# Zero-padding the low part of the keys to 128 rows, and regrouping ScalarE and VectorE in the turning of x

## The chip, the cores and the metric

The kernel runs on one core of one Trainium2 chip. The metric is the device time of one execution in microseconds (us). Three runs of the kernel before took 1794.21, 1795.99 and 1801.98 us; their median, 1795.99 us, is the time before.

## The reference

Two layers over 256 tokens of 2048 channels, in float32. The first layer projects the normalized input once and feeds a convolution module and a sparse attention with 16 heads in 4 groups; the second is a causal pooling mixer. After each comes an MLP. The part that the change touches is the scores of the attention, and the transposition of the residual x ahead of the MLPs and of the pooling layer:

```python
sc = jnp.einsum('bqgrd,bngd->bgrqn', qb, kc) * scale            # compressed keys
ss = jnp.einsum('bqgrd,bgqkld->bgrqkl', qb, ks_sel) * scale     # selected keys
sw = jnp.einsum('bqgrd,bkgd->bgrqk', qb, kwb) * scale           # window keys
...
x = x + even_mixer(x, ...)
x = x + mlp(x, ...)      # rmsnorm(x) @ w1, squared ReLU, @ w2
x = x + odd_mixer(x, ...)
x = x + mlp(x, ...)
```

With 256 tokens all blocks are selected and the window covers everything, so that the selected and the window branch are two plain causal attentions with keys of their own.

## The kernel before

**Products in two halves.** A float32 product is made from operands rounded to a faster format (F32R) and their remainders: a tensor `hi` holds the rounded values, `lo` the difference, and three matmuls (hi by hi, hi by lo, lo by hi) stand for one. ScalarE rounds (`nc.scalar.activation(hi, ..., AF.Copy)`), VectorE subtracts. The weights stream from HBM in units of 1 MB (`wraw`), are split into `whi` and `wlo` (L147, and L78, which is the line of every VectorE instruction, since a helper counts their cost), and are used two units later. Matmuls stand under L194, transposes on TensorE under L232.

**Order of the work.** Each engine runs its instructions in the order in which the program issues them. In the mixing part, `unit_cols` (L365) multiplies one unit of weights with xT in four quarters, and after each quarter `beside` (L356) issues a quarter of the split of a later unit, then as many taps of the convolution (`ctile`, VectorE) as the meter `vector.t` allows against the time counted for TensorE, then one entry of the list `steps`. In the part with the queries (L859, 8 units of q) the entries are the steps of the attention.

**A step of the attention** (`step`, L678). There are 32, one for each pair of heads, half and token block; step s transposes the softmax numerators of step s-2 (`T<-ident,p`), forms the scores of step s (`scores`, L609), and multiplies the values of step s-4 (`PV`). The scores of both branches are three matmuls into one bank `S`: the query `q`, whose 128 rows hold the rounded query in one half and its remainder in the other, with `kk2`, which holds the rounded keys twice (L616); the rounded half of the query alone, 64 rows, with `klo`, the remainder of the keys (L617); and a product with the identity that adds the causal mask (L618, `cmaskr`). A step with the second token block is wide (512 columns, both branches over 256 keys), one with the first is narrow (256 columns). VectorE takes the maximum (`nb`), ScalarE the exponentials (`p`), and two steps later TensorE transposes them. `klo` and `kk2` are written in `keys_values` (L475), in the stretch from 134 to 174 us: two units for each of two branches.

**Buffers.** Tiles of one tag rotate through `bufs` buffers, and the writer waits for the readers of the tile that had the buffer before. `row` has 4 buffers, `ln` has 3.

**Turning x** (`turn_x`, L242). Four calls ahead of the first MLP (from 367 us), four ahead of the pooling layer and four ahead of the second MLP (from 1043 to 1125 us). A call turns 512 channels: 8 transposes into two banks of PSUM, then for each of 4 tiles a rounding by ScalarE (L254) and a difference by VectorE, both reading the bank and scaling by `g`. Between the calls, in the pooling part, VectorE adds the pooled parts to x (`pt`, then `x<-x,pt`), and the next transposes wait for that x.

Of the kernel before, what the change touches and what calls it, by code (L numbers as in the profile page):

```python
# [27 lines left out]
F32 = mybir.dt.float32  # L28
F32R = mybir.dt.float32r
AF = mybir.ActivationFunctionType  # L30
ALU = mybir.AluOpType
# [3 lines left out]
P = 128  # L35
S = 256
# [143 lines left out]
def trunk(ctx: ExitStack, tc: tile.TileContext, a: dict, out: bass.AP, dump: dict | None = None):  # L180
    nc = tc.nc
# [6 lines left out]
    vector = Meter(nc.vector)  # L188
    pe = [0.0]

    def mm(out, w, x, **kw):
        n = int(np.prod(x.shape[1:]))
        pe[0] += max(4 * n / 2400, 0.214) if x.dtype == F32 else max(n / 2400 + 0.0025, 0.107)
        nc.tensor.matmul(out, w, x, **kw)  # L194
# [39 lines left out]
    def split_evac(hi, lo, src):  # L234
        nc.scalar.activation(hi, src, AF.Copy)
        vector.tensor_sub(lo, src, hi.bitcast(F32))
# [5 lines left out]
    def turn_x(dc, g0, bank):  # L242

        xT[dc] = act.tile([P, 4, 512], F32R, tag="xT", bufs=4, name="xT")
        for h in range(2):
            t = bank().rearrange("p (f t) -> p f t", f=2)
            for f in range(2):
                d = (4 * dc + 2 * h + f) * P
                for tok in range(2):
                    transpose(t[:, f, tok * P:(tok + 1) * P], x[:, tok, d:d + P])  # L250
            for f in range(2):
                dt = 4 * dc + 2 * h + f
                o, g = xT[dc][:, 2 * h + f], vec[:, g0 + dt:g0 + dt + 1]
                nc.scalar.activation(o[:, 0:256], t[:, f], AF.Copy, scale=g)  # L254
                vector.scalar_tensor_tensor(o[:, 256:512], t[:, f], g, o[:, 0:256].bitcast(F32),
                                            op0=ALU.mult, op1=ALU.subtract)

    def by_token(acc, X, hi, lo, first, last, between=None, outer=False):

# [13 lines left out]
    with ExitStack() as mx:  # L273
        mix = mx.enter_context(tc.tile_pool(name="mix", bufs=1, side="right", reuse_waits="tile"))
# [38 lines left out]
            vector.tensor_add(sq[0][:, 0:n], sq[0][:, 0:n], sq[0][:, n:2 * n])  # L313
        nc.scalar.activation(identr, ident, AF.Copy)
        r0 = const.tile([P, 2], F32, name="r0")
        rbc = mix.tile([P, S], F32, name="rbc")
        pss = acc1(2)

        def start_steps():
# [107 lines left out]
        for ct in range(1, 8):  # L427
            g, a_ = acc1(), acc1()
# [16 lines left out]
        for i in range(2):  # L445
            t = mix.tile([P, KT, P], F32, tag="q8", bufs=2, name="w1")
# [5 lines left out]
        for i in range(2):  # L452
            t = mix.tile([P, 512], F32, tag="tt", bufs=3, name="wgl")[:, 0:384]
# [7 lines left out]
        for pr in range(2):  # L461
            for i in range(2):
                acc = acc1()
# [5 lines left out]


        kk2 = mix.tile([P, 2, 2, 2, 256], F32R, name="kk2")
        klo = mix.tile([P, 2, 2, 256], F32R, name="klo")
        v = mix.tile([P, 2, 2, 256], F32, name="v")

        def keys_values(br):  # L475
            for i in range(2):
                acc = acc1()
                unit_cols(acc)
                hi = mix.tile([P, 256], F32R, tag="row", bufs=4, name="khi")
                split_evac(hi, klo[:, i, br], acc)  # L480
                for h in range(2):
                    for o in range(2):
                        nc.scalar.activation(kk2[64 * o:64 * o + 64, i, h, br], hi[64 * h:64 * h + 64].bitcast(F32), AF.Copy)
            accs = [acc1() for _ in range(2)]
            for u in range(2):
                hi, lo = W.next(8)
                for tok in range(2):
                    for k in range(8):
                        mm3_toks(accs[tok], xT[2 * u + k // 4], k % 4, hi[:, k], lo[:, k], tok,
                                 u == 0 and k == 0, u == 1 and k == 7)  # L490
                        if k % 4 == 3:
                            beside(2 * tok + k // 4)
            for tok in range(2):
                nc.scalar.activation(v[:, br, tok], accs[tok], AF.Copy)
# [105 lines left out]
        qT, Pt, Tt, SM, PV, PC, PP, ab = {}, {}, {}, {}, {}, {}, {}, {}  # L600
# [8 lines left out]
        def scores(s):  # L609

            j, half, tok = of_step(s)
            n = P * (tok + 1)
            b = slice(64 * half, 64 * half + 64)
            S_ = bank("S")[:, 0:2 * n].rearrange("p (b k) -> p b k", b=2)
            q = qT[j][:, half, tok * P:(tok + 1) * P]
            mm(S_, q, kk2[:, j // 4, half, :, 0:n], start=True, stop=False)  # L616
            mm(S_, q[b], klo[b, j // 4, :, 0:n], start=False, stop=False)  # L617
            mm(S_[:, :, n - P:n], identr, cmaskr[:, None].to_broadcast([P, 2, P]), start=False, stop=True)  # L618
            if s % 4 == 0:
                SM[j] = const.tile([P, 2, 2, 2], F32, tag="sums", bufs=4, name="sums")  # L620
            nb = const.tile([P, 2], F32, tag="nb", bufs=3, name="nb")
            p = mix.tile([P, 2, n], F32, tag="p", bufs=3, name="p", padded_shape=[P, 2, 256])
            vector.tensor_reduce(nb, S_, axis=AX, op=ALU.max, negate=True)

            def exps():
                for br in range(2):
                    nc.scalar.activation(p[:, br], S_[:, br], AF.Exp, bias=nb[:, br:br + 1],
                                         accum_out=SM[j][:, tok, half, br:br + 1])
                return p
            Pt[s] = exps  # L630
# [64 lines left out]
        def cmp_scores(j):  # L695
            m, r = divmod(j, 4)
            transposed()
            sc = (ab.pop(j)[:, 256:384] if j < 7 else bank("T")[:, 0:128]).rearrange("p (t h i n) -> p t h i n", t=2, h=2, i=2)
            for tok in range(2):
                for half in range(2):  # L700
                    mm(sc[:, tok, half], qT[j][:, half, tok * P:(tok + 1) * P], kcT[:, m, half],
                       start=(tok == 0 and half == 0), stop=True, skip_group_check=True)
            if r == 0:

                PC[m] = mix.tile([P, 2, 2, 4, 16], F32, tag="scm", bufs=1, name="scm")
            lo = const.tile([P, 2, 2, 16], F32, tag="sclo", bufs=2, name="sclo")
            nc.scalar.activation(lo, sc[:, :, :, 1], AF.Copy)
            pc = PC[m][:, :, :, r]
            vector.tensor_add(pc, sc[:, :, :, 0], lo)
            vector.tensor_add(pc, pc, madd[:, :, None].to_broadcast([P, 2, 2, 16]))  # L710

        def cmp_max(m):
            PP[m] = mix.tile([P, 2, 2, 4, 32], F32, tag="pp", bufs=1, name="pp")
            nc.gpsimd.memset(PP[m], 0.0)
            cm = const.tile([P, 16], F32, tag="cm", bufs=2, name="cm")
            s3 = PC[m].rearrange("p t h r n -> p (t h r) n")
            vector.tensor_reduce(cm, s3, axis=AX, op=ALU.max)
            vector.tensor_tensor(s3, s3, cm[:, :, None].to_broadcast([P, 16, 16]), op=ALU.subtract)
# [44 lines left out]
        ln = {}  # L763
# [95 lines left out]
        for j in range(8):  # L859
# [19 lines left out]
            m = j // 4  # L879
# [540 lines left out]
```

## Time and profile before

| | |
|---|---|
| runs | 1794.21, 1795.99, 1801.98 us |
| median | 1795.99 us |
| the profiled execution, its time | 1794.04 us |
| the same, span from first to last instruction | 1792.3 us |
| granted TensorE clock, mean | 0.998 |
| TensorE busy | 1767.5 us, 99% of the span |
| VectorE busy | 1517.0 us, 85% |
| ScalarE busy | 1088.4 us, 61% |
| GpSimd busy | 57.8 us, 3% |

The profile is of one execution. PE is TensorE's matmuls, PEld its loads of stationary operands, DVE is VectorE, ACT ScalarE, POOL GpSimd. Matmuls are pipelined, and the end of one is modelled; what a matmul takes from the engine is therefore read from the distance between its start and the start of the next. A TensorE that is 99% busy by its records can still lose time between two starts.

### The profile page before, as it was taken

To read this page: it belongs to the slowest core of one execution; us is meant where nothing else is said; L and a number is where in the kernel's file an instruction comes from. 1 tells how busy PE (TensorE), PEld (TensorE's weight loads), DVE (VectorE), ACT (ScalarE), POOL (GpSimd) and SP (SyncE) were. 2 spreads that over 40 slices of the span, in tenths; PEclk is the share of its full clock that TensorE was granted. 3 is DMA by queue.
4 is the path that set the end of the run, shared out by engine and by line. 5 is a ranking of instruction groups with operands and counts; after the bars stand their busy time and mean duration, and the time that the engine had idled before them with its cause. 6 is when DMAs were issued, how large, how long until landed. Compare 5 with 4: busy or idle time off the path is not lost.

```text
span 1792.3 us, 28698 instructions
## 1 busy us (share of the span) xinstructions
PE 1767.5 (99%) x11726; PEld 1599.5 (89%) x11726; DVE 1517.0 (85%) x1884; ACT 1088.4 (61%) x1626; POOL 57.8 (3%) x78
## 2 busy tenths in 40 slices
PE   9999999999999999999999999999999999999997
PEld 7999988889898988999898988989889998989885
DVE  6998896865889898988989868698999889898984
ACT  4446565546666666666656655766666666666663
POOL 1000000000000000000000000000000000000000
PEclk9999999999999999999999999999999999999999
DMA  7654322545787787878787764678877787878872
GB/s 276 238 187 143 117 75 103 202 183 200 239 250 257 255 263 238 251 235 278 236 285 235 217 227 162 212 253 255 256 238 247 233 291 236 270 235 258 245 239 104
DMA packets 58052, 399.89 MB, mean 223 GB/s; under 512 B 6560, under 2 KB 6960, under 8 KB 10816
## 3 DMA queue, kind: packets, MB, share of 16 engines
q1 hardware_dynamic: 47760, 333.47, 48.4%
q0 software_dynamic: 8576, 61.43, 18.4%
q10 hardware_dynamic: 1584, 3.16, 0.5%
q8 instruction: 92, 1.51, 0.3%
q14 instruction: 40, 0.33, 0.0%
HBM read 395.93 MB, written 2.10 MB: 222 GB/s over the span
## 4 chain that ended last, share of the span: by engine, by line
PE 72%; DVE 22%; ACT 3%; issue 2%; DMA 1%; ACTq 0%; POOLq 0%; SPq 0%; DVEq 0%
PE acc L194 68%; DVE wlo L78 11%; DVE z L78 3%; DVE s L78 3%; PE S L194 2%; DVE x L78 2%; ACT whi L147 1%; PE PV L194 1%; PE T L232 1%; DVE xT L78 1%; DVE f L78 1%; DMA xraw<-in_xT 0%; ACT xT L254 0%; ACT t L1018 0%; ACT sq L997 0%
## 5 line engine op out<-in xcount | busy, mean ns | idle before, releaser
L194 PE MATMUL acc<-xT,whi 128*128 128x256 f32 x4992 | 874.1, 279 | 0.3
L194 PEld LDWEIGHTS acc<-xT,whi 128*128 128x128 f32 x4992 | 765.8, 188 | 10.5 <-DVE xT L78 0.7
L78 DVE TENSOR_TENSOR wlo<-wraw,whi 128x1024 fp32r<-128x1024 f32 (+1 forms) x552 | 604.0, 1124 | 146.4 <-ACT whi L147 145.3
L194 PE MATMUL acc<-xT,wlo 128*128 128x256 f32 x2496 | 694.9, 278 | 0.0
L147 ACT ACTIVATE whi<-wraw 128x1024 fp32r<-128x1024 f32 (+1 forms) x552 | 514.5, 973 | 94.7 <-PE acc L194 66.2
L194 PEld LDWEIGHTS acc<-xT,wlo 128*128 128x128 f32 x2496 | 470.8, 189 | 0.0
L194 PE MATMUL acc<-whi,s 128*128 128x512 f32 x960 | 318.6, 393 | 2.7 <-DVE s L78 1.6
L78 DVE TENSOR_TENSOR wlo<-z,whi 128x1024 fp32r<-128x1024 f32 x224 | 266.6, 1216 | 48.3 <-ACT whi L147 47.2
L147 ACT ACTIVATE whi<-z 128x1024 fp32r<-128x1024 f32 x224 | 230.6, 1054 | 93.8 <-DVE z L78 75.9
L194 PE MATMUL acc<-whi,f 128*128 128x512 f32 x864 | 283.1, 392 | 0.0
L194 PEld LDWEIGHTS acc<-whi,s 128*128 128x128 f32 x960 | 179.5, 188 | 42.0 <-DVE s L78 7.4
L1017 ACT ACTIVATE t<-acc 128x256 f32<-128x256 f32 x128 | 48.8, 382 | 252.9 <-PE acc L194 252.4
L194 PE MATMUL acc<-wlo,s 128*128 128x512 f32 x480 | 190.8, 398 | 1.2
L194 PEld LDWEIGHTS acc<-whi,f 128*128 128x128 f32 x864 | 162.5, 188 | 32.1
L194 PE MATMUL acc<-wlo,f 128*128 128x512 f32 x432 | 169.5, 392 | 0.0
L78 DVE SCALAR_TENSOR_TENSOR x<-acc,r,x 128x512 f32<-128x512 f32 x156 | 115.5, 742 | 13.5 <-PE acc L194 13.5
L194 PEld LDWEIGHTS acc<-wlo,s 128*128 128x128 f32 x480 | 90.2, 188 | 28.1 <-DVE wlo L78 9.7
L78 DVE SCALAR_TENSOR_TENSOR ctile<-ctile,cw 128x256 f32<-128x256 f32 x240 | 101.6, 476 | 0.0
L194 PEld LDWEIGHTS acc<-wlo,f 128*128 128x128 f32 x432 | 81.2, 188 | 16.0
L1062 ACT ACTIVATE s<-s 128x512 fp32r<-128x512 f32 x56 | 35.4, 632 | 72.1 <-DVE s L78 72.1
L78 DVE TENSOR_TENSOR z<-z,b 128x1024 f32<-128x1024 f32 x56 | 65.9, 1218 | 0.0
L78 DVE TENSOR_TENSOR z<-z,wraw 128x1024 f32<-128x1024 f32 x56 | 65.8, 1214 | 0.0
(205 smaller groups left out, 1366.4 us busy)
## 6 DMA issues: line engine op xcount, KB each, us to landing
wraw<-in_ws SPq DMA_DIRECT2D x254, 1024.0 KB, 6.1
z<-in_ws SPq DMA_DIRECT2D x28, 1024.0 KB, 7.5
b<-in_ws SPq DMA_DIRECT2D x28, 1024.0 KB, 4.8
b<-in_ws POOLq DMA_DIRECT2D x28, 1024.0 KB, 8.9
z<-in_ws POOLq DMA_DIRECT2D x28, 1024.0 KB, 8.0
xraw<-in_xT SPq DMA_DIRECT2D x4, 512.0 KB, 7.6
wraw<-in_ws SPq DMA_DIRECT2D x8, 256.0 KB, 7.6
w<-in_cmp_w POOLq DMA_DIRECT2D x2, 1024.0 KB, 7.4
```

Source lines behind the costliest of these rows:

```text
L78: return fn(*args, **kw)
L147: nc.scalar.activation(hi[:, c], raw[:, c], AF.Copy)
L194: nc.tensor.matmul(out, w, x, **kw)
L232: nc.tensor.transpose(out, src, ident[0:n, 0:n])
L1017: nc.scalar.activation(out, acc, AF.Relu)
L1062: nc.scalar.activation(F[tag][:, :, 0:P], src(), AF.Copy)
```

## The change

The remainder of the keys gets a tile of twice the size with one more index, the half (the group of 64 channels). For each half, the 64 rows of the other half are zero, and the matmul takes all 128 rows of the query; the zeros meet the query's remainder. GpSimd sets the zeros once, and VectorE writes each remainder in two instructions of 64 rows. Three tiles that had buffers of their own get buffers of a rotating tag: `rbc` and `scm` in `row`, `pp` in `ln`. In `turn_x` the four differences are issued after the four roundings of the call.

```diff
     def turn_x(dc, g0, bank):
         xT[dc] = act.tile([P, 4, 512], F32R, tag="xT", bufs=4, name="xT")
+        rest = []
...
                 nc.scalar.activation(o[:, 0:256], t[:, f], AF.Copy, scale=g)
-                vector.scalar_tensor_tensor(o[:, 256:512], t[:, f], g, o[:, 0:256].bitcast(F32),
-                                            op0=ALU.mult, op1=ALU.subtract)
+                rest.append(lambda o=o, t=t[:, f], g=g: vector.scalar_tensor_tensor(
+                    o[:, 256:512], t, g, o[:, 0:256].bitcast(F32), op0=ALU.mult, op1=ALU.subtract))
+        for r in rest:
+            r()
...
-        rbc = mix.tile([P, S], F32, name="rbc")
+        rbc = mix.tile([P, S], F32, tag="row", bufs=4, name="rbc")
...
-        klo = mix.tile([P, 2, 2, 256], F32R, name="klo")
+        klo = mix.tile([P, 2, 2, 2, 256], F32R, name="klo")
+        for h in range(2):
+            nc.gpsimd.memset(klo[64 - 64 * h:128 - 64 * h, :, h].bitcast(F32), 0.0)
...
-                split_evac(hi, klo[:, i, br], acc)
+                nc.scalar.activation(hi, acc, AF.Copy)
+                for h in range(2):
+                    b = slice(64 * h, 64 * h + 64)
+                    vector.tensor_sub(klo[b, i, h, br], acc[b], hi[b].bitcast(F32))
...
-            b = slice(64 * half, 64 * half + 64)
...
-            mm(S_, q[b], klo[b, j // 4, :, 0:n], start=False, stop=False)
+            mm(S_, q, klo[:, j // 4, half, :, 0:n], start=False, stop=False)
...
-                PC[m] = mix.tile([P, 2, 2, 4, 16], F32, tag="scm", bufs=1, name="scm")
+                PC[m] = mix.tile([P, 2, 2, 4, 16], F32, tag="row", bufs=4, name="scm")
...
-            PP[m] = mix.tile([P, 2, 2, 4, 32], F32, tag="pp", bufs=1, name="pp")
+            PP[m] = mix.tile([P, 2, 2, 4, 32], F32, tag="ln", bufs=3, name="pp")
```

TensorE issues the same matmuls in the same order as before, 32 of them with 128 rows for 64. On VectorE, where the second branch of the keys is written (`keys_values(1)`, L475), the program issues the following; `klo` is the remainder of the keys, `ctile` a tap of the convolution, `wlo` the split of a unit of weights. Before:

```order
L78 TENSOR_TENSOR klo<-acc,khi 128x256
L78 SCALAR_TENSOR_TENSOR ctile<-ctile,cw 128x256 x2
L78 TENSOR_TENSOR wlo<-wraw,whi 128x1024
L78 SCALAR_TENSOR_TENSOR ctile<-ctile,cw 128x256 x4
L78 TENSOR_TENSOR wlo<-wraw,whi 128x1024
```

With the change:

```order
L78 TENSOR_TENSOR klo<-acc,khi 64x256 x2
L78 SCALAR_TENSOR_TENSOR ctile<-ctile,cw 128x256
L78 TENSOR_TENSOR wlo<-wraw,whi 128x1024
L78 SCALAR_TENSOR_TENSOR ctile<-ctile,cw 128x256 x4
L78 TENSOR_TENSOR wlo<-wraw,whi 128x1024
```

The remainder is two instructions, the meter counts both, and one tap moves to a later quarter; after this the taps of the attention's part stand one place later than before.

In `turn_x` no engine's own order changes; what each instruction waits for does. On ScalarE, the first two calls ahead of the first MLP (L254 is the rounding, PE_49 and DVE_49 are the signals of TensorE and VectorE). Before:

```order
L254 ACTIVATE xT<-acc,vec 128x256 [waits PE_49]
L254 ACTIVATE xT<-acc,vec 128x256 [waits DVE_49]
L254 ACTIVATE xT<-acc,vec 128x256 [waits PE_49]
L254 ACTIVATE xT<-acc,vec 128x256 [waits DVE_49]
L147 ACTIVATE whi<-wraw 128x512 x2
L147 ACTIVATE whi<-wraw 128x512 [waits DMAHW2_49,PE_49,Activation_49]
```

With the change:

```order
L255 ACTIVATE xT<-acc,vec 128x256 [waits PE_49]
L255 ACTIVATE xT<-acc,vec 128x256
L255 ACTIVATE xT<-acc,vec 128x256 [waits PE_49]
L255 ACTIVATE xT<-acc,vec 128x256
L147 ACTIVATE whi<-wraw 128x512 x2
L147 ACTIVATE whi<-wraw 128x512 [waits DMAHW2_49,DVE_49,PE_49]
```

The second rounding of each bank no longer waits for VectorE's difference in that bank. On VectorE, the differences of the first call with what stands around them, before (each waits for a rounding):

```order
L78 TENSOR_TENSOR wlo<-wraw,whi 128x512 [waits DMAHW1_49,Activation_49]
L78 TENSOR_TENSOR wlo<-wraw,whi 128x512 [waits Activation_49]
L78 SCALAR_TENSOR_TENSOR xT<-acc,vec,xT 128x256 [waits Activation_49] x4
L78 TENSOR_TENSOR wlo<-wraw,whi 128x512 [waits Activation_49] x2
L78 TENSOR_TENSOR x<-xt,acc 128x512
```

and with the change:

```order
L78 TENSOR_TENSOR wlo<-wraw,whi 128x512 [waits DMAHW1_49,Activation_49]
L78 TENSOR_TENSOR wlo<-wraw,whi 128x512 [waits Activation_49]
L78 SCALAR_TENSOR_TENSOR xT<-acc,vec,xT 128x256 [waits PE_49,Activation_49]
L78 SCALAR_TENSOR_TENSOR xT<-acc,vec,xT 128x256
L78 SCALAR_TENSOR_TENSOR xT<-acc,vec,xT 128x256 [waits PE_49,Activation_49]
L78 SCALAR_TENSOR_TENSOR xT<-acc,vec,xT 128x256
L78 TENSOR_TENSOR wlo<-wraw,whi 128x512 [waits Activation_49] x2
L78 TENSOR_TENSOR x<-xt,acc 128x512
```

The first difference of a bank now waits for both roundings of that bank, and the second for nothing.

## Rows read from the trace of the kernel before

**Rows 1.** The page: busy time of the engines (part 1), and the chain of work that ended last, by engine (part 4).

```profile
PE 1767.5 (99%) x11726; PEld 1599.5 (89%) x11726; DVE 1517.0 (85%) x1884; ACT 1088.4 (61%) x1626; POOL 57.8 (3%) x78
...
PE 72%; DVE 22%; ACT 3%; issue 2%; DMA 1%; ACTq 0%; POOLq 0%; SPq 0%; DVEq 0%
```

**Rows 2.** Busy time by stretch: length of the stretch, then PE, PEld, DVE, ACT, POOL busy (with the number of instructions), granted clock, DMA share, GB/s. The first stretch is the projection of the convolution's channels, the second the attention, the third the part of the attention in which taps of the convolution still run beside it.

```profile
36.00:134.00 98.00, 98.00 (x829) 97.87 (x828) 93.10 (x168) 44.56 (x62) 5.14 (x11) 1.00 0.62 231
...
194.00:300.00 106.00, 104.30 (x747) 90.84 (x746) 87.25 (x203) 67.49 (x214) 0.53 (x1) 1.00 0.27 95
...
194.00:274.00 80.00, 79.98 (x587) 70.72 (x586) 71.75 (x168) 51.03 (x159) 0.53 (x1) 1.00 0.26 93
```

**Rows 3.** Timeline of TensorE, one wide step (from 225.26) and one narrow step (from 228.73): start, duration, engine, line, instruction, out<-in, rows*columns of the stationary operand, out shape, count, and idle time before it.

```profile
225.26 0.48 PE L194 MATMUL S<-kk,q 128*128 128x512 f32 x1
...
225.67 0.49 PE L194 MATMUL S<-klo,q 64*128 64x512 f32 x1
...
226.09 0.19 PEld L194 LDWEIGHTS S<-cmaskr,identr 128*128 128x128 f32 x1 [0.24 <-issue]
226.09 0.39 PE L194 MATMUL S<-cmaskr,identr 128*128 128x256 f32 x1
...
226.31 1.00 PE L194 MATMUL PV<-v,tt 128*128 128x64 f32 x8
...
228.73 0.36 PE L194 MATMUL S<-kk,q 128*128 128x256 f32 x1
...
229.02 0.38 PE L194 MATMUL S<-klo,q 64*128 64x256 f32 x1
...
229.33 0.39 PE L194 MATMUL S<-cmaskr,identr 128*128 128x256 f32 x1
...
229.55 0.55 PE L194 MATMUL PV<-v,tt 128*128 128x64 f32 x4
```

**Rows 4.** Timeline of TensorE where every matmul has 128 rows: the product with w_out, 512 columns (the first of these follows PV), and a unit of the queries, 256 columns.

```profile
227.56 0.39 PE L194 MATMUL acc<-xT,whi 128*128 128x256 f32 x2
...
227.79 0.28 PE L194 MATMUL acc<-xT,wlo 128*128 128x256 f32 x1
...
290.85 0.48 PE L194 MATMUL acc<-whi,yo 128*128 128x512 f32 x1
291.16 0.39 PE L194 MATMUL acc<-wlo,yo 128*128 128x512 f32 x1
291.39 0.63 PE L194 MATMUL acc<-whi,yo 128*128 128x512 f32 x2
```

**Rows 5.** Who VectorE waited for between 195 and 274 us: instruction <- releaser: us in total, times, longest.

```profile
DVE nb L78 <- PE S L194: 3.0, 6, 0.8
DVE q L78 <- ACT q L870: 1.5, 1, 1.5
DVE o_tok L78 <- PE T L194: 1.1, 1, 1.1
DVE scm L78 <- ACT sclo L707: 0.6, 1, 0.6
```

**Rows 6.** Timeline of three engines around 251 to 259 us: `scm` reads the bank into which the next unit's `acc` is formed; `nb` and `p` belong to the scores whose `p` is transposed at 258.69.

```profile
251.57 0.21 DVE L78 TENSOR_TENSOR scm<-acc,sclo 128x64 f32<-128x64 f32 x1
...
253.75 0.69 DVE L78 TENSOR_REDUCE nb<-S 128x2 f32<-128x512 f32 x1
...
254.39 0.48 PE L194 MATMUL acc<-xT,whi 128*128 128x256 f32 x2
...
256.61 0.47 ACT L627 ACTIVATE p<-S,nb 128x256 f32<-128x256 f32 x1
...
258.69 0.60 PE L232 MATMUL T<-ident,p 128*128 128x128 f32 x4
```

**Rows 7.** Instructions by tile, with shortest, median and longest duration in ns, first and last start (`klo`, and `q`, an instruction of VectorE with 64 rows and 256 columns); the page's group of the convolution's taps (busy us, mean ns); and who VectorE waited for between 134 and 190 us.

```profile
L194 PE MATMUL S<-klo,q x32: 379/437/501, 194.7 to 298.3; 64*128 64x512 f32 x16, 64*128 64x256 f32 x16
L78 DVE TENSOR_TENSOR klo<-acc,khi x4: 410/420/426, 135.0 to 172.7; 128x256 fp32r<-128x256 f32 x4
...
L78 DVE SCALAR_TENSOR_TENSOR q<-acc,q x16: 417/422/426, 193.8 to 285.9; 64x256 fp32r<-64x256 f32 x16
...
L78 DVE SCALAR_TENSOR_TENSOR ctile<-ctile,cw 128x256 f32<-128x256 f32 x240 | 101.6, 476 | 0.0
...
DVE wlo L78 <- ACT whi L147: 8.8, 7, 2.8
```

**Rows 8.** Timeline of ScalarE and VectorE in one call of `turn_x` in the pooling part.

```profile
1103.39 0.48 ACT L254 ACTIVATE xT<-acc,vec 128x256 fp32r<-128x256 f32 x1 [1.04 <-PE acc L232]
...
1106.26 0.47 DVE L78 SCALAR_TENSOR_TENSOR xT<-acc,vec,xT 128x256 fp32r<-128x256 f32 x1
...
1106.77 0.84 ACT L254 ACTIVATE xT<-acc,vec 128x256 fp32r<-128x256 f32 x2 [2.90 <-DVE xT L78]
1107.28 0.88 DVE L78 SCALAR_TENSOR_TENSOR xT<-acc,vec,xT 128x256 fp32r<-128x256 f32 x2 [0.54 <-ACT xT L254]
...
1108.70 0.48 DVE L78 SCALAR_TENSOR_TENSOR xT<-acc,vec,xT 128x256 fp32r<-128x256 f32 x1 [0.55 <-ACT xT L254]
```

**Rows 9.** Who TensorE's loads waited for between 1040 and 1130 us (total us, times, longest); `acc L232` are the transposes of x, `acc L194` the matmuls that read xT.

```profile
PEld acc L232 <- DVE x L78: 1.5, 2, 1.0
PEld acc L194 <- DVE xT L78: 0.7, 2, 0.3
```

## The prediction

> **What bounds the kernel now.** I read the page first, then busy time by stretch, then timelines of the two places that the change touches. TensorE is busy for 99% of the span, and the chain that ended last runs through it for 72% and through VectorE for 22% [rows 1]. So a saving counts only if it shortens TensorE's own list or a wait of TensorE. The stretches say what kind of bound it is [rows 2]. From 36 to 134 us TensorE starts 829 matmuls in 98.00 us, 0.118 us each, and its loads are busy for 97.87 us: nothing else fits there. In the attention, 194 to 300 us, it is busy for 104.30 of 106 us, but starts only 747 matmuls, 0.142 us each, and its loads are busy for 90.84 us. Something there takes time that is neither a matmul nor a load, and the timeline shows what [rows 3].
>
> A wide step: the starts of `kk`, `klo`, `cmaskr` and the first `PV` lie at 225.26, 225.67, 226.09 and 226.31, so the three score matmuls take 0.41, 0.42 and 0.22 us, 1.05 in all. A narrow step takes 0.29, 0.31 and 0.22, 0.82 in all. Where every matmul has 128 rows, one with 512 columns takes 0.23 us (291.16 to 291.39), or 0.31 where it comes first after matmuls of another kind (290.85 to 291.16), and one with 256 columns 0.115 us (two in 0.23, from 227.56) [rows 4]. The excess stands at the two passages into the 64 rows of `klo` and out of them. The load ahead of `cmaskr` starts together with its matmul, after 0.24 us of "issue" [rows 3]; elsewhere a load runs during the matmul before.
>
> **The change part by part.**
>
> *The scores.* TensorE's list is the same but for the 64 rows, which become 128. If all three are then like the matmuls of [rows 4], a wide step takes 0.31 + 0.23 + 0.115 = 0.66 us for 1.05, and a narrow one, with the same 0.08 for coming first, 0.08 + 3 x 0.115 = 0.43 for 0.82. Both save 0.39 us, and 32 steps [rows 7] save 12.5 us. Bounds: `cmaskr` repeats its moving operand for both branches, and its 0.22 us may be its own; then a step saves 0.29 us, and all 9.3. If nothing of 0.08 is left, 0.41 to 0.42 and 13.3. I take 12.5: since the load ahead of `cmaskr` starts only with its matmul, its 0.22 us holds a load that otherwise is hidden.
>
> [...]
>
> *VectorE falls behind.* This is the cover that wears thin. Between 194 and 274 us, where taps of the convolution still run, VectorE is busy for 71.75 of 80 us [rows 2], and its waits over a noticeable length are 3.0 us for scores and 3.2 for other things [rows 5]. So its list takes 80 - 6.2 = 73.8 us. The moved tap adds 0.42 us (101.6 us over 240) [rows 7]: 74.2. TensorE's list becomes 80 - 24 x 0.39 = 70.6 us, with 24 of the 32 steps ahead of 274. VectorE is then 3.6 us late at the end, and what counts is whether TensorE sees it. Worst is 254 us: 19 steps have saved 7.4 us, plus 0.4, less the waits that VectorE can drop until then (3.0 + 0.6): 4.2 us behind. The margin there: `nb` ends at 254.44, two exponentials of 0.47 follow, and with starting up `p` could be ready at 255.6; its transposes start at 258.69 [rows 6], 3.1 us later, of which a narrow step between takes 0.39. So about 1.5 us of waiting. `scm` gives the same: it ends at 251.78, the matmul that needs its bank starts at 254.39 [rows 6], 2.6 us of margin less a wide step, against 3.8 us of lateness: 1.6. I take 1.6 us, once, since TensorE's waiting gives VectorE the time back, and after 274 VectorE's list gets short. Bounds: 0 (if `p` and `scm` come sooner than that) to 6.8 us (if VectorE can drop only its 3.0 us of waits for scores: it then leaves 3.0 - 0.4 = 2.6 us of the 24 steps' 9.4).
>
> *TensorE's own rate.* A dense run of 256-column matmuls goes at 0.118 us each [rows 2], one after a pause at 0.115 [rows 4]. With the pauses gone, some 200 matmuls of the units between the steps may go at the slower rate: 200 x 0.003 = 0.6 us lost. Bounds 0 and 1.
>
> *Writing the remainders.* Four instructions of 128 rows (0.42 us) become eight of 64. The nearest row is `q`, 64 rows and 256 columns, 0.42 us too [rows 7], so 4 x 0.42 = 1.7 us more on VectorE between 134 and 174 us. VectorE waits there for ScalarE's roundings for 8.8 us [rows 7], and these cover it: 0. If the cover were gone, +1.7. GpSimd's zeros are two instructions more on an engine whose 78 took 57.8 us in all [rows 1], 0.7 us each, and no instruction of VectorE or TensorE waits for GpSimd that did not before: 0, and 1.5 us if all of it were on the path. The three moved tiles add waits on tiles read long before: 0. ScalarE's and VectorE's new waits for older signals (`whi` now waits for DVE_49) are for instructions that lie units back: 0.
>
> *The turning of x.* In a late call VectorE's four differences run from 1106.26 to 1109.18, 2.92 us, with two waits of 0.54 for a rounding that itself waited for a difference; ScalarE had made the first rounding at 1103.39 and then sat still for 2.90 us [rows 8]. With all roundings done, four differences take 3 x 0.40 + 0.48 = 1.7 us: 1.2 us less on VectorE. Where VectorE is there first, it starts a rounding later (0.37, from two in 0.84) and ends about 0.9 sooner (one alternation for each bank less). What TensorE loses around these calls is small: 1.5 us for x and 0.7 us for xT between 1040 and 1130 us, four waits [rows 9]. Three of the four calls from 1095 us on give 1.2 us each, more than these 2.2 us need. I take 2.0; bounds 0 and 2.2. The calls before the first MLP cost TensorE nothing now, and give nothing.
>
> **Sum.** Against the profiled execution's 1794.04 us: -12.5 + 1.6 + 0.6 - 2.0 = -12.3, giving 1781.7. The median of the runs is 1795.99, 1.95 higher, and less 12.3 it is 1783.7. I forecast **1783 us**. The parts' bounds, short of VectorE taking over, give savings from 15.5 down to 6.7 us, both ends unlikely since they need every part on one side; I give this case 1779 to 1788.
>
> **The rivals.**
> *VectorE takes over.* Its 3.2 us of other waits between 194 and 274 cannot be dropped [rows 5], and TensorE gains there only 2.6 us; the 8 later steps give 3.1 and the turning 2.0: -7.7, 1788.3 from the median. For it: VectorE's 71.75 of 80 us. Against: its results are due two steps later, not at once.
> [...]
> *Slower: VectorE's list sets the pace at both places.* It has 1.7 us more between 134 and 174, 0.4 of the tap, and starts five calls of the turning (1079 to 1125 us) 0.37 later each, 1.9: +4.0, 1800. This decides only if VectorE's 8.8 us of waits there turn out as chains that it cannot shorten, if TensorE's saving all turns into waits for VectorE, and if the later differences aren't sooner. [Rows 8] speak against the last.
> *The change in the turning does nothing*, because no engine's order changes, only what is waited for: then 2.0 us are missing, 1785, inside the forecast's own range.
>
> **How the numbers follow.** Forecast 0.70, VectorE takes over 0.14, pauses stay 0.12, slower 0.04. About 0.5%, 9 us, is what a measurement of this kernel can tell from no change, so faster means below 1787. The forecast holds that for nearly all its range (0.68), VectorE's case for some (0.06): faster 0.74; the rest of them and the pauses' case: within, 0.22; slower 0.04. The range reaches from 1778 (full savings, and a run a little below) to 1790 (VectorE's case whole), and leaves out the pauses' and the slower case, 0.16.
>
> **What would show it.** In the changed profile `klo` has 128*128 rows, the "issue" time ahead of `klo` and `cmaskr` is gone, and a wide step takes about 0.66 us from `kk` to the next start, a narrow one 0.43. If these stand at 1.05 and 0.82, the account of the passages is wrong. Busy time from 194 us to the end of the attention should shrink by some 11 us with the same matmuls; TensorE should show one or two new waits, 1 to 2 us, for `p` or `scm` near 245 to 260, and VectorE's waits for scores should vanish. More waits than 4 us there mean that VectorE took over. In `turn_x` the two roundings of a bank should follow each other, and TensorE's waits for x and xT near 1100 us should be under 0.5 us.

## The result, and the profile after

The changed kernel takes **1777.9 us** (median; 1775.47 to 1779.22), the kernel before, measured beside it, 1795.1 us (1790.65 to 1801.98). The ratio is 0.991, with an interval from 0.9892 to 0.9928: 13 to 19 us faster. The profiled execution took 1777.96 us, with a span of 1776.2 us. Forecast were 1783 us and a saving of 12.3; the saving in the two profiled spans is 16.1.

The page of the changed kernel: busy time, and the chain that ended last by engine.

```profile
PE 1752.6 (99%) x11726; PEld 1595.4 (90%) x11726; DVE 1518.5 (85%) x1888; ACT 1084.6 (61%) x1626; POOL 59.7 (3%) x80
...
PE 78%; DVE 18%; ACT 2%; issue 1%; DMA 1%; ACTq 0%; POOLq 0%; SPq 0%; DVEq 0%
```

TensorE is busy for the same 99% of its span, with the same 11726 matmuls [rows 1]: the time has gone out of the distances between them. Busy time by stretch (columns as in [rows 2]):

```profile
36.00:134.00 98.00, 98.00 (x829) 97.87 (x828) 95.42 (x168) 44.58 (x62) 7.04 (x13) 1.00 0.62 231
194.00:300.00 106.00, 104.32 (x816) 99.58 (x815) 95.37 (x224) 71.45 (x226) 0.53 (x1) 1.00 0.30 105
```

In the first stretch TensorE's work did not move; VectorE is busy for 2.3 us more there with the same 168 instructions, which is taken up below. From 194 to 300 us TensorE now starts 816 matmuls where it started 747, and its loads are busy for 99.58 us where it was 90.84 [rows 2]. One wide and one narrow step (TensorE's timeline, columns as in [rows 3]):

```profile
227.20 0.48 PE L194 MATMUL S<-kk,q 128*128 128x512 f32 x1
227.52 0.39 PE L194 MATMUL S<-klo,q 128*128 128x512 f32 x1
227.75 0.28 PE L194 MATMUL S<-cmaskr,identr 128*128 128x256 f32 x1
227.87 1.00 PE L194 MATMUL PV<-v,tt 128*128 128x64 f32 x8
...
230.28 0.37 PE L194 MATMUL S<-kk,q 128*128 128x256 f32 x1
230.48 0.28 PE L194 MATMUL S<-klo,q 128*128 128x256 f32 x1
230.60 0.28 PE L194 MATMUL S<-cmaskr,identr 128*128 128x256 f32 x1
230.72 0.55 PE L194 MATMUL PV<-v,tt 128*128 128x64 f32 x4
```

From `kk` to `PV` it is 0.67 and 0.44 us, where it was 1.05 and 0.82 [rows 3]. The whole attention, from the first `kk` to the last `cmaskr`, first of before, then of the change:

```profile
194.31 0.50 PE L194 MATMUL S<-kk,q 128*128 128x512 f32 x1
...
298.57 0.39 PE L194 MATMUL S<-cmaskr,identr 128*128 128x256 f32 x1
```

```profile
194.44 0.50 PE L194 MATMUL S<-kk,q 128*128 128x512 f32 x1
...
286.55 0.28 PE L194 MATMUL S<-cmaskr,identr 128*128 128x256 f32 x1
```

That is 104.26 us, and then 92.11: **12.15 us less**. The second place is the turning of x. The transposes of the fourth and of the eighth of the late groups, before and then with the change:

```profile
1078.33 1.03 PE L232 MATMUL acc<-ident,x 128*128 128x128 f32 x8
...
1119.80 1.09 PE L232 MATMUL acc<-ident,x 128*128 128x128 f32 x8
```

```profile
1065.96 1.03 PE L232 MATMUL acc<-ident,x 128*128 128x128 f32 x8
...
1105.47 1.04 PE L232 MATMUL acc<-ident,x 128*128 128x128 f32 x8
```

41.47 us became 39.51, 1.96 less, and the 0.7 us of waits for xT [rows 9] behind these calls are gone too: some **2.5 us**. In a call ScalarE and VectorE no longer alternate; this is the call at 1091 us:

```profile
1090.87 1.20 ACT L255 ACTIVATE xT<-acc,vec 128x256 fp32r<-128x256 f32 x3
...
1092.74 1.65 DVE L78 SCALAR_TENSOR_TENSOR xT<-acc,vec,xT 128x256 fp32r<-128x256 f32 x4
```

The four differences take 1.65 us in one piece, where they took 2.92 [rows 8]. The two places make 14.6 us of the 16.1; where the rest lies is a question for the experiments.

### The profile page after: what moved, and what is told of

It is laid out like the page before. It is cut to its first block, busy times and chain, and to the rows that moved or that the text cites. A ratio compares the mean times of both kernels' runs of the same rounds, so it can differ in the third digit from the quotient of the medians.

```text
span 1776.2 us, 28729 instructions
## 1 busy us (share of the span) xinstructions
PE 1752.6 (99%) x11726; PEld 1595.4 (90%) x11726; DVE 1518.5 (85%) x1888; ACT 1084.6 (61%) x1626; POOL 59.7 (3%) x80
## 4 chain that ended last, share of the span: by engine, by line
PE 78%; DVE 18%; ACT 2%; issue 1%; DMA 1%; ACTq 0%; POOLq 0%; SPq 0%; DVEq 0%
PE acc L194 73%; DVE wlo L78 9%; DVE z L78 3%; DVE s L78 3%; PE S L194 2%; DVE x L78 2%; PE PV L194 1%; ACT whi L147 1%; PE T L232 1%; PE acc L232 1%; DVE f L78 0%; DMA xraw<-in_xT 0%; ACT t L1026 0%; DMA ident<-in_ident 0%; ACT t L1025 0%
## 5 line engine op out<-in xcount | busy, mean ns | idle before, releaser
L194 PE MATMUL acc<-xT,whi 128*128 128x256 f32 x4992 | 872.1, 279 | 0.0
L194 PEld LDWEIGHTS acc<-xT,whi 128*128 128x128 f32 x4992 | 764.8, 188 | 10.1
L194 PE MATMUL acc<-xT,wlo 128*128 128x256 f32 x2496 | 694.0, 278 | 0.0
L194 PEld LDWEIGHTS acc<-xT,wlo 128*128 128x128 f32 x2496 | 470.7, 189 | 0.0
L194 PE MATMUL acc<-whi,s 128*128 128x512 f32 x960 | 318.5, 393 | 2.8 <-DVE s L78 1.6
L194 PE MATMUL acc<-whi,f 128*128 128x512 f32 x864 | 283.0, 392 | 0.0
L194 PEld LDWEIGHTS acc<-whi,s 128*128 128x128 f32 x960 | 179.3, 188 | 42.2 <-DVE s L78 7.5
L194 PE MATMUL acc<-wlo,s 128*128 128x512 f32 x480 | 190.8, 397 | 1.1
L194 PEld LDWEIGHTS acc<-whi,f 128*128 128x128 f32 x864 | 162.4, 188 | 32.2
L194 PE MATMUL acc<-wlo,f 128*128 128x512 f32 x432 | 169.4, 392 | 0.0
L194 PEld LDWEIGHTS acc<-wlo,s 128*128 128x128 f32 x480 | 90.1, 188 | 28.2 <-DVE wlo L78 9.7
L194 PEld LDWEIGHTS acc<-wlo,f 128*128 128x128 f32 x432 | 81.1, 188 | 16.0
```

## The experiments

The account at this point: the scores gave 12 us by the two passages of each step, the turning 2.5 us, and all else is hidden. Its rivals: part of the 12 us is from the moved taps and tiles; each 64-row matmul is slow by itself, and passages have no price; the turning does nothing, or more than the trace shows; VectorE still has cover, or has none.

**The scores alone** (the change without this part of its diff):

```diff
-        rest = []
...
-                rest.append(lambda o=o, t=t[:, f], g=g: vector.scalar_tensor_tensor(
-                    o[:, 256:512], t, g, o[:, 0:256].bitcast(F32), op0=ALU.mult, op1=ALU.subtract))
-        for r in rest:
-            r()
+                vector.scalar_tensor_tensor(o[:, 256:512], t[:, f], g, o[:, 0:256].bitcast(F32),
+                                            op0=ALU.mult, op1=ALU.subtract)
```

> The changed kernel with the turning of x as before. Theory (the passages between 64 and 128 rows cost 0.39 us a step, the turning gives 2.5 us by itself): 12.1 us faster than before, about 1783, with a wide step's three score matmuls in 0.66 us and a narrow one's in 0.43, and TensorE's loads still waiting for VectorE's x and xT around 1100 us, about 2 us. Rival (the two parts help each other, or part of the gain is from elsewhere): less than 10 or more than 14 us.

1781.43 us, ratio 0.993 (0.9908 to 0.9952): 9 to 16.5 us faster. In its trace the attention goes from 194.42 to 286.55 us, 92.13, the same as with the whole change, and the turning is as slow as before: 0.41 and 0.79 us of waits for x.

```profile
1092.05 0.98 PE L232 MATMUL acc<-ident,x 128*128 128x128 f32 x7 [0.41 <-DVE x L78]
...
1101.25 0.98 PE L232 MATMUL acc<-ident,x 128*128 128x128 f32 x7 [0.79 <-DVE x L78]
```

The parts don't help each other: the theory holds.

**The turning alone**, twice:

```diff
+        rest = []
...
-                vector.scalar_tensor_tensor(o[:, 256:512], t[:, f], ...
+                rest.append(lambda o=o, t=t[:, f], g=g: vector.scalar_tensor_tensor(...
+        for r in rest:
+            r()
```

> The kernel before with only the four differences of a call issued after its four roundings. Theory: TensorE's waits for x and xT around 1100 us go, 2.0 to 2.5 us, and nothing changes before the attention's end: about 1792.8. Rival (no engine's order changes, so it does nothing): within 0.5 us of before, with the waits for x and xT still there. By the first theory the stretch from 1040 to 1130 us holds no wait of TensorE over 0.3 us.

1789.95 us, ratio 0.997 (0.9957 to 0.9983): 3.1 to 7.7 us faster, so the rival that it does nothing falls. In the trace no wait for x or xT is left, and the same transposes as above stand 39.51 us apart, as with the whole change:

```profile
1076.64 1.03 PE L232 MATMUL acc<-ident,x 128*128 128x128 f32 x8
...
1116.15 1.04 PE L232 MATMUL acc<-ident,x 128*128 128x128 f32 x8
```

But the time says more than 2.5 us. So it was measured again (the 2.1 in the text below should have read 3.1):

> The kernel before with the turning of x alone changed, a second time, because the first measurement (2.1 to 7.7 us faster) reached far beyond the 2.5 us that its trace shows between 1095 and 1130 us. Theory (the gain is those 2.5 us, the rest was chance in where the slower stretches of TensorE lay): the two measurements together hold 2.5 us, and the new one is nearer to it. Rival (the turning gives 5 us, half of it in a place that the trace of one execution does not show): again 4.5 us or more.

1788.99 us, ratio 0.9979 (0.9959 to 0.9998): 0.4 to 7.4 us, middle 3.8. This one holds 2.5 us, the first doesn't, and the middle of both is above 4. Something is worth a further 1 to 3 us that no wait of TensorE shows.

**What the change does on VectorE, without its gain**: everything of the scores' part but the 128 rows, with the turning of x as before.

```diff
+            b = slice(64 * half, 64 * half + 64)
...
-            mm(S_, q, klo[:, j // 4, half, :, 0:n], start=False, stop=False)
+            mm(S_, q[b], klo[b, j // 4, half, :, 0:n], start=False, stop=False)
```

> The changed kernel's remainder of the keys (large tile, GpSimd's zeros, two instructions of 64 rows, the moved taps, the tags), but its score matmul again takes only the 64 rows of its half, and the turning of x is as before. Theory (all of this is hidden, the gain is from the 128 rows alone): within 0.5 us of before, 1795, wide step 1.05 and narrow 0.82 us. Rival (part of the gain is from where taps and tiles now lie): 2 to 5 us faster. Rival on the other side (VectorE's 1.7 us more shows): 1 to 2 us slower.

1796.04 us, ratio 1.0001 (0.9986 to 1.0016), and steps of 1.06 and 0.83 us (225.33 to 226.39, 228.79 to 229.62); the wide one:

```profile
225.33 0.48 PE L194 MATMUL S<-kk,q 128*128 128x512 f32 x1
...
226.39 1.00 PE L194 MATMUL PV<-v,tt 128*128 128x64 f32 x8
```

Taps and tiles gave nothing that shows within the interval's 2.9 us, and VectorE's extra instructions are hidden. Its profiled execution lost 3 us in the attention, all at one place, which is told at the end.

**Where the price of 64 rows lies**: `klo`'s matmul of the kernel before twice in a row (the remainder of the keys then counts twice), and the mask's product ahead of it.

```diff
             mm(S_, q[b], klo[b, j // 4, :, 0:n], start=False, stop=False)
+            mm(S_, q[b], klo[b, j // 4, :, 0:n], start=False, stop=False)
```

> The kernel before with the 64-row matmul of klo issued twice in a row in each of the 32 steps, so the remainder of the keys counts twice in the scores. Theory (the price is in the passages into 64 rows and out of them): the second one costs only its pitch, 0.23 us with 512 and 0.115 with 256 columns, 16 x 0.23 + 16 x 0.115 = 5.5 us, about 1800.6, and in the timeline the two starts lie 0.23 apart in a wide step. Rival (each 64-row matmul is itself slow, 0.42 and 0.31 us): 16 x 0.42 + 16 x 0.31 = 11.7 us, about 1807.

```diff
-            mm(S_, q[b], klo[b, j // 4, :, 0:n], start=False, stop=False)
-            mm(S_[:, :, n - P:n], identr, cmaskr[...], start=False, stop=True)
+            mm(S_[:, :, n - P:n], identr, cmaskr[...], start=False, stop=False)
+            mm(S_, q[b], klo[b, j // 4, :, 0:n], start=False, stop=True)
```

> The kernel before with the mask's product ahead of the 64-row matmul of klo, so the order in a step is kk, cmaskr, klo, PV. Theory (a price at each passage into 64 rows and out of them, whatever is next to it): the two passages only move, cmaskr costs 0.115 to 0.13 us, klo and what follows it carry the rest, and the time stays within 0.5% of before, a step by 0.1 us or less. Rival (the price is from klo following kk directly, or only from the load of the identity): steps get 0.1 to 0.3 us shorter, 3 to 9 us in all.

Twice: 1801.74 us, ratio 1.0031 (1.0013 to 1.005), 5.6 us by its middle; its attention runs from 190.71 to 300.45, 109.74 us, **5.48 more** than before, where 5.5 and 11.7 were expected. Mask first: 1793.49 us, ratio 1.0002 (0.9986 to 1.0018). A wide step of each:

```profile
230.15 0.48 PE L194 MATMUL S<-kk,q 128*128 128x512 f32 x1
230.56 0.73 PE L194 MATMUL S<-klo,q 64*128 64x512 f32 x2
231.22 0.39 PE L194 MATMUL S<-cmaskr,identr 128*128 128x256 f32 x1
231.44 1.00 PE L194 MATMUL PV<-v,tt 128*128 128x64 f32 x8
```

```profile
228.39 0.48 PE L194 MATMUL S<-kk,q 128*128 128x512 f32 x1
228.70 0.28 PE L194 MATMUL S<-cmaskr,identr 128*128 128x256 f32 x1
228.91 0.50 PE L194 MATMUL S<-klo,q 64*128 64x512 f32 x1
229.33 1.10 PE L194 MATMUL PV<-v,tt 128*128 128x64 f32 x8
```

Two `klo` take 0.66 us for one's 0.42: the second costs 0.24, the pitch of 512 columns. With the mask first, `kk` takes 0.31 (0.41 before), as with the change, where 128 rows follow too (0.32); the matmul that stands ahead of `klo`, now `cmaskr`, takes 0.10 more than its 0.115; and what follows `klo`, now `PV`, is 0.10 longer. So a passage into 64 rows costs 0.10 us, at the matmul ahead of it. The way out costs 0.19 at `klo` (0.42 less 0.23) and 0.10 at the matmul behind it. Together 0.39, in either order. That each 64-row matmul is slow by itself falls.

**VectorE's cover**: one more addition of 0.21 us ahead of each maximum, on both kernels.

```diff
+        extra = const.tile([P, 64], F32, name="extra")
+        nc.gpsimd.memset(extra, 0.0)
...
+            nc.vector.tensor_add(extra[:, 0:64], extra[:, 0:64], extra[:, 0:64])
             vector.tensor_reduce(nb, S_, axis=AX, op=ALU.max, negate=True)
```

> The kernel before with one more addition of 128 x 64 (0.21 us, on a tile of its own) on VectorE ahead of each of the 32 maxima, 6.7 us in all, 5.0 of them in the 24 steps up to 274 us. Theory (any of VectorE's 6.2 us of waits between 195 and 274 us goes when VectorE comes later): these waits shrink to 1 to 2 us, TensorE waits for nothing new, and the time is within 0.5% of before. Rival (the 3.2 us of waits that are not for scores stay, as the prediction's case of VectorE taking over had it): they are still 3 us, the lateness grows by 2 us, and TensorE waits 1 to 2 us for p or scm.

> The changed kernel with the same addition ahead of each maximum. Theory (VectorE's cover between 194 and 262 us is used up by the change to the last 0.5 us, since 0.4 us of its waits are left there and p comes 0.1 us ahead of its transposes): 5.0 us in 24 steps less 0.5 to 1.0 become waits of TensorE for p, scm or q, so about 4 us slower than the changed kernel, 1782. Rival (there is still cover: TensorE's order has slack that the trace does not show): no new waits, within 1 us of the changed kernel.

On the kernel before: 1793.01 us, ratio 0.9998 (0.9985 to 1.0011). TensorE's waits in the attention don't change. Who VectorE waited for between 195 and 274 us:

```profile
DVE q L78 <- ACT q L874: 1.0, 1, 1.0
DVE nb L78 <- PE S L194: 0.9, 2, 0.5
DVE o_tok L78 <- PE T L194: 0.7, 1, 0.7
DVE scm L78 <- ACT sclo L711: 0.6, 1, 0.6
```

3.2 us in all, where it was 6.2 [rows 5]: waits for scores fell by 2.1 and the others by 0.9. The theory had 1 to 2 us left, so this part of it missed; the rival's waits of TensorE did not come either. An addition is worth less than its record of 0.22 us: in most steps VectorE starts its next instruction 0.135 us after it, so that 24 of them take some 3.2 us, and the waits fell by 3.0. On the changed kernel: 1779.42 us, ratio 0.9917 (0.9903 to 0.993). The time is 1.5 us above that of the change, within what runs differ by, but the place shows it: the attention goes from 190.89 to 285.92 us, 95.03, **2.92 more** than with the change alone, and TensorE's loads have waits that were not there (190 to 290 us, columns as in [rows 9]):

```profile
PEld acc L194 <- DVE scm L78: 1.4, 2, 1.1
PEld T L194 <- DVE o_tok L78: 0.7, 1, 0.7
PEld T L232 <- ACT p L639: 0.5, 2, 0.3
PEld S L194 <- DVE q L78: 0.4, 1, 0.4
```

The same additions cost nothing before and 2.9 us with the change: VectorE's cover is used up. That was the theory; its 4 us counted each addition at its full record.

**The changed kernel again**, since its spans differ from run to run by more than its parts:

> The changed kernel once more, to learn what one execution differs from another by. Theory (the profile of the change lost 4.5 us and gained 5.9 against that of before through stretches in which TensorE goes 0.113 or 0.118 us from one 256-column matmul to the next, and where such a stretch lies is chance): the stretches lie elsewhere than in the first profile, the time is 1776 to 1783 by median, the waits of TensorE are the same to 0.5 us, and no stretch between 20 us and the last 30 us has a granted clock under 1. Rival (the stretches belong to the program): they lie at the same places, and the time is within 1 us of 1777.9.

1776.5 us, ratio 0.9901 (0.9884 to 0.9918). The stretch from 800 to 860 us in the first profile of the change and in this one:

```profile
800.00:860.00 60.00, 60.00 (x401) 54.80 (x400) 52.19 (x54) 37.11 (x48) 2.56 (x3) 1.00 0.81 260
```

```profile
800.00:860.00 60.00, 60.00 (x386) 54.48 (x385) 51.24 (x53) 37.12 (x47) 2.56 (x3) 1.00 0.78 250
```

One program, at places 2 us apart in it, no wait, the same granted clock, and 4% fewer matmuls: in such stretches TensorE goes 0.118 us from one 256-column matmul to the next, in the others 0.113. Where they lie differs between executions.

**Fewer slow stretches with the new turning?** Each timeline was gone through for groups of three such matmuls behind 400 us that took 0.34 us or 0.353. As before and as changed, one profile each:

> The kernel before, profiled once more. In the timelines so far, of the groups of three 256-column matmuls behind 400 us that took either 0.34 or 0.353 us, 541 to 783 were slow in the six profiles with the turning of x as before, and 382 to 582 in the six with it changed; 185 groups at 0.0135 us would be 2.5 us. Theory (the changed turning leaves fewer slow stretches behind it): over 600 slow groups. Rival (chance): anywhere from 380 to 780.

> The kernel before with the turning of x alone changed, profiled once more, for the same count. Theory (fewer slow stretches): under 500 slow groups, and at least 100 fewer than the kernel before in this call. Rival (chance): anywhere from 380 to 780, and no order between the two.

The counts in these texts are lower than the trace's own starts give, which are finer than the timeline's 0.01 us. Counted from them (two matmuls by `whi` and one by `wlo`, 0.340 or 0.353 us to the next start), there are 891 slow groups in the one (1796.2 us) and 461 in the other (1788.88 us, one run each): the theory's way. Over all profiles of the study, seven without the new turning have 686 to 1002, 848 in the mean, and seven with it 349 to 767, 577 in the mean. The ranges overlap.

These groups close the account. In all fourteen profiles the time from the last score product to the last instruction is, by a fit of three numbers, 1485.0 us, plus 0.0126 us for each slow group, less 2.44 us where the turning is changed; no profile lies more than 0.3 us off. So the turning itself is worth the 2.5 us that the waits show, and what goes beyond lies in slow groups alone, 271 in the mean or 3.4 us.

Whether the new turning makes them fewer is less sure. The level changes only at certain places of the program, the same in all profiles, from 450 us on mostly 552 matmuls or some 84 us apart; of the 16 sections between them 4 to 7 are slow without the new turning, and 1 to 5 with it. The two sections behind the first calls of `turn_x` are slow in 11 of 14 cases without it and in 3 of 14 with it, the others in 28 of 98 and 19 of 98, which can be chance.

**Yo a quarter earlier.** One wait of TensorE's in the attention stood through all this: 1.68 us for `q` in the last query unit, since ScalarE and VectorE make a part of `yo` first.

```diff
-                steps[2] = both(steps[2], one(o_transposed, 0, 0))
-                steps[3] = both(steps[3], one(o_transposed, 0, 1))
+                steps[1] = both(steps[1], one(o_transposed, 0, 0))
+                steps[2] = both(steps[2], one(o_transposed, 0, 1))
```

> The changed kernel with the two transpositions of the first heads' output, and the roundings and differences of yo behind them, issued one quarter of the last query unit earlier. Theory (TensorE's one wait left in the attention, 1.68 us for q, comes from VectorE and ScalarE making yo ahead of q): the wait falls to under 0.4 us, TensorE waits for nothing else instead, and the attention ends 1.3 to 1.7 us earlier against the start of that unit, about 1775.5 by median. Rival (VectorE has no time to give a quarter earlier either): a wait for p, scm or yo of about the same length stands there, and nothing is gained.

1774.2 us, ratio 0.9904 (0.9883 to 0.9925). The matmul that waits for `q`, in the change and then here:

```profile
276.28 0.47 PE L194 MATMUL acc<-whi,yo 128*128 128x512 f32 x1 [1.68 <-DVE q L78]
```

```profile
276.17 0.47 PE L194 MATMUL acc<-whi,yo 128*128 128x512 f32 x1 [0.18 <-DVE q L78]
```

The attention goes from 195.83 to 286.44, 90.61 us: 1.50 less than with the change, and no new wait: the theory's way. The kernel beats that of before by 17 us; against the change the times alone can't tell 1.5 us.

## Why the prediction was right, step by step

The direction and the mechanism were right, and 12.3 us was too small. The time, 1777.9 us, lies at the low end of the range (1778), and the 17.2 us between the medians are more than the 15.5 that the bounds of the parts allowed. That it did not fall further out is luck: it turned on slow stretches of TensorE, which no part of the sum had.

- *The scores*: forecast 12.5 and steps of 0.66 and 0.43; measured 12.15, 0.67 and 0.44. The split into passages was right too, by the doubled `klo`. By klo_twice and klo_last the way in costs 0.10 us and the way out 0.29. With the change, `klo` and `cmaskr`, 128 rows each and with stationary operands of their own, take 0.115 to 0.12 us per 256 columns, and their loads are hidden: in the wide step of the profile after, that of `klo` runs from 227.29 to 227.48 us, and that of `cmaskr` from 227.52 to 227.71, each during the matmul before.
- *VectorE falls behind*: forecast 1.6 us of waiting, measured none. The step that failed is the lateness of 4.2 us at 254 us. From the first `kk` to the start of the `nb` in [rows 6], VectorE runs the same instructions before and with the change (busy time by stretch, columns as in [rows 2]; before, then the change):

```profile
194.31:253.75 59.44, 59.44 (x435) 52.32 (x435) 54.33 (x128) 38.51 (x121) 0.00 (x0) 1.00 0.26 91
```

```profile
194.44:249.05 54.61, 54.61 (x458) 53.68 (x458) 53.24 (x128) 38.19 (x123) 0.00 (x0) 1.00 0.28 99
```

  It took 4.83 us less, where the forecast let it drop 3.6 us of waits and added 0.4 for the moved tap. It dropped 3.7 us of idle time and was busy for 1.1 us less, which no row of waits announced, and the moved tap is not among these instructions. So the `nb` ran 4.70 us earlier (249.05 for 253.75), and the transposes behind it 7.60 (251.09 for 258.69): 2.9 us late, not 4.2. The margin, 2.7 us in the forecast, was mis-sized by little: the last `p` ends at 251.07 and its transposes start at 251.09.

```profile
250.61 0.46 ACT L635 ACTIVATE p<-S,nb 128x256 f32<-128x256 f32 x1
...
251.09 0.60 PE L232 MATMUL T<-ident,p 128*128 128x128 f32 x4
```

  No wait is seen, and at most 0.2 us of cover is left (the first two of the four transposes take the earlier half of `p`); the added load then showed that the cover is gone. Behind 254 us VectorE's waits for `q` and `o_tok` went too, which the upper bound of 6.8 us and the rival of VectorE taking over had as lasting. Of [rows 5] this is left with the change between 195 and 274 us:

```profile
DVE nb L78 <- PE S L194: 0.4, 1, 0.4
```

- *TensorE's own rate*: forecast 0.6 us lost, measured nothing of the kind: the attention lost 0.35 us to the forecast of the steps in all. The step that failed is the reading of 0.118 and 0.115 us [rows 2, 4] as dense and less dense. The rate has two levels that come in stretches.
- *Writing the remainders*: forecast 0 under cover of VectorE's waits for roundings. Those fell from 8.8 [rows 7] to 6.9 us between 134 and 190 us, and halves_only took no more time. Right in the sum, but the zeros were not free. GpSimd's two instructions took 0.95 us each, not 0.7, and the forecast put their effect on VectorE at nothing, since no instruction waits for GpSimd. Yet while GpSimd sets zeros (until 44.67 us, 42.65 before), two instructions of VectorE last 3.57 us that took 0.96 before:

```profile
41.25 3.57 DVE L78 TENSOR_SCALAR ctile<-ctile,cw,vec 128x256 f32<-128x256 f32 x2
```

  In halves_only they last 2.79, and VectorE's cover hides it: TensorE starts 829 matmuls from 36 to 134 us, as before. Why they last longer was not tested.
- *The turning of x*: forecast 2.0, bounds 0 and 2.2. The waits gave 2.5, above the upper bound, which had counted TensorE's waits alone. A further 1 to 3 us, by the times of the turning alone, go with fewer slow stretches of TensorE. They are clearest behind the calls ahead of the first MLP, which the forecast said would give nothing. How the one causes the other was not found, so for that part only a link is shown, and the counts alone leave room for chance.
- The sum by places is 12.15 + 2.5 = 14.6, for the forecast's 12.3: 1.6 of the difference is the wait that did not come, 0.6 the rate, 0.5 the turning, and the scores gave 0.35 less. The two profiled spans differ by 16.1, since TensorE's two rates lie differently in them: 686 slow groups before and 569 with the change, 1.5 us. The same work in the first MLP, of before and then of the change, 309 matmuls in 36 us and 318:

```profile
404.00:440.00 36.00, 36.00 (x309) 36.00 (x308) 16.92 (x20) 23.94 (x44) 0.00 (x0) 1.00 0.53 205
```

```profile
392.00:428.00 36.00, 36.00 (x318) 35.92 (x317) 17.89 (x21) 23.93 (x45) 0.00 (x0) 1.00 0.53 205
```

  Between the medians of the runs the difference is 17.2.
- *The rivals*: that VectorE takes over fell by the waits that did not last; that the pauses ahead of `klo` and `cmaskr` stay (its chance 0.12), by the steps of 0.67 and 0.44 us; slower, by halves_only and the turning alone; that the turning does nothing, by the turning alone.

## What to carry to other kernels

Look at the distance between starts, not at busy time: a 64-row matmul among 128-row ones costs 0.39 us here for the way in and out, so rows of zeros came out cheaper than the smaller tile (12.15 us over 32 steps), where the operand exists anyway and the zeros are set once. When a bound engine gets faster, count all waits of the engine behind it as slack, not only those for the one that got faster (of 6.2 us of VectorE's, 0.4 were left here), and then look at what is left: here at most 0.2 us around 251 us, so the next microsecond saved up to there needs VectorE as well. Where several engines read one bank in turn, issue all of one engine's reads before the other's (2.4 us here).

## What the runs showed of the hardware that was not expected

**Two rates.** Matmuls of 256 columns go at 0.113 or 0.118 us each, at one granted clock (1.00 in both); the longest slow stretch behind 400 us is 254 us (536 to 790 us in the profile of the change). In the MLPs every change from fast to slow behind 450 us stands right behind a pause of TensorE of 0.10 to 0.81 us among the products with 512 columns, but fast sections follow such pauses too; the change at 404 us in the kernel before stands behind the eight transposes of the last call of `turn_x`. From 36 to 134 us eleven of the fourteen profiles start 824 to 830 matmuls (before 829 [rows 2]); klo_twice had this, and klo_last and load_after had 858:

```profile
36.00:134.00 98.00, 98.00 (x859) 97.87 (x858) 95.20 (x175) 47.70 (x69) 5.18 (x11) 1.00 0.65 239
```

Their attention began some 3.5 us earlier (190.71 to 190.89, for 194.09 to 194.59 in ten others and 195.83 in yo_earlier), though klo_twice and klo_last issue the same as the kernel before up to there. What sets the level is open; it is part of why runs of one kernel lie 10 us apart.

**A fall of the clock in one execution.** In the profile of halves_only, behind the wait of 1.68 us for `q` (284.82 to 286.50 us) and with 17 matmuls started in the 5 us around it, the granted clock was 0.84, and 0.50 in the next 5 us:

```profile
285.00:290.00 5.00, 3.50 (x17) 2.89 (x17) 2.44 (x5) 3.47 (x13) 0.00 (x0) 0.84 0.22 92
290.00:295.00 5.00, 5.00 (x16) 3.93 (x16) 2.69 (x6) 1.79 (x6) 0.00 (x0) 0.50 0.00 0
```

It cost some 3 us: its attention took 107.29 us (194.42 to 301.71) for 104.26. The same wait stands in the other profiles but yo_earlier's, and none of them shows a fall there (in that of the kernel before, 19 matmuls started from 285 to 290 us, at a clock of 1.00).
